# Expert weights stored tile by tile: one row of 8 KB per partition instead of two of 4 KB

## The chip, the core and the metric

The kernel runs on one core of one Trainium2 chip. The metric is the device time of one execution in microseconds (us). Three runs of the kernel before took 1865.32, 1869.44 and 1870.21 us; the median, 1869.44 us, is what is compared.

## What is computed

Two layers of a token mixer and a mixture of experts, for 512 latent tokens and 256 context tokens of width 1024, in float32. Almost all of the bytes that the kernel reads are the experts' weights. Cut to that part, the reference is:

```python
def expert_choice_ffn(xn, w_router, w_gate, w_up, w_down):
    cap = EC_CAPACITY_FACTOR * n // N_EXPERTS
    aff = jax.nn.softmax(jnp.einsum('bnd,de->bne', xn, w_router), axis=-1)
    gate, idx = lax.top_k(jnp.swapaxes(aff, 1, 2), cap)
    xs = xn[bidx, idx]
    hid = jax.nn.silu(jnp.einsum('becd,edf->becf', xs, w_gate)) * jnp.einsum('becd,edf->becf', xs, w_up)
    ys = jnp.einsum('becf,efd->becd', hid, w_down) * gate[..., None]
    return jnp.zeros_like(xn).at[bidx, idx].add(ys)
```

There are 16 experts per layer, each with three matrices of 1024 x 1024 (4 MB each): 2 x 16 x 12 MB in all. Each expert takes 64 latent tokens. In the first layer it also takes 32 context tokens; the last layer computes latent tokens alone.

## The kernel before

Experts are worked on in eight pairs per layer. A matrix of one expert comes in four tiles of 1 MB: tile i holds rows 256 i to 256 i + 255, two rows per partition (row 256 i + p and row 256 i + 128 + p in partition p). One pair therefore takes 24 tiles: four for each of three matrices and two experts.

The tiles of a layer stand in one list, `wq` (L1129 to L1132), in the order in which they are used: gate and up of pair 0, then for each pair gate of the next, down of this one, up of the next. `load_experts` (L1135) issues the loads on SP's DMA queue in that order, each into the next of a ring of buffers, `wreg`, and it issues one as soon as the tile that had the buffer is used up. In the last layer there are 16 buffers of 8 KB per partition: nine from L1128, six that come free at L1191 and one at L1710. In the first layer the ring is made of the four of L1191 and those added at L1715. The loads of the first tiles start before the routing is known.

`wide` (L1419) is the product of a pair with one matrix: for each of the four tile pairs, the latent tokens' matmuls (L1433), a filler, the context tokens' matmuls in the first layer (L1443), then `load_experts` again. The fillers are small pieces of other work put in between by hand: transposes and token gathering of the next pair (L1379, L1382), transposes of the hidden values (L1485), the scattering of the results (L1498, L1499).

Two stretches are special. The last down product of the last layer, `down_last` (L1662, matmuls at L1693), takes its weights by columns instead: each of the last two experts' down matrices comes as four tiles of 256 columns, so that a partition takes eight rows of 1 KB (L1138 to L1143; the fourth tile comes in two halves). And in the first layer the results of the first six pairs are added up in device memory by POOL's scattering DMAs (L1537), and read back once, also on POOL's queue (`collect`, L1546 and L1548), for transposes at L1554 and L1566 that stand as fillers among the matmuls of the last pairs. PE works strictly in order, so that a filler that waits holds up the matmuls behind it.

`layout` (L1763) arranges the inputs on the host, before the measured time. It passes the experts' matrices on as they are. The DMA engines' shares: 16 engines move each tile together, and an engine's record in the trace is a packet.

Of the kernel before, what the change touches and what calls it, by code (L numbers as in the profile page):

```python
# [14 lines left out]
D = 1024  # L15
KB = 8
# [3 lines left out]
E = 16  # L20
# [135 lines left out]
def build(nc, tc, xT, ctxT, params, w_ada, w_gates, w_in, w_out, w_router, w_e_gate, w_e_up, w_e_down,  # L156
# [3 lines left out]
    pe, act, dve, pool, sp = nc.tensor, nc.scalar, nc.vector, nc.gpsimd, nc.sync  # L160


    def body(A, RB, PS, scr, xrow, acc):
# [3 lines left out]
        def V(reg, *shape, dt=F32, off=0):  # L167
            n = 1
            for s in shape:
                n *= s  # L170
            k = 2 if dt == BF16 else 1
            assert off + n // k <= reg[1], (off, n, reg)
            ap = reg[2].tile[:, reg[0] + off:reg[0] + off + n // k]
            if dt == BF16:
                ap = ap.bitcast(dt)
            if len(shape) > 1:
                names = "abcdefg"[:len(shape)]
                ap = ap.rearrange("p (" + " ".join(names) + ") -> p " + " ".join(names),
                                  **{names[i]: shape[i] for i in range(1, len(shape))})
            return ap  # L180

        def B(i):
            return PS[:, i, :]
# [86 lines left out]
        def after(inst, firsts, how=mybir.DependencyClass.Sync):  # L270

            for f in firsts:
                tc.add_manual_dep(inst.ins, f.ins.name, mybir.DependencyInfo(how, mybir.DependencyReason.DATA),
                                  reason="its turn comes later")
# [122 lines left out]
        for l in range(2):  # L397
# [198 lines left out]
            for s in seqs:  # L596
                o, n = OFF[s], LEN[s]
# [5 lines left out]
            for q in range(4):  # L603
                sl = slice(32 * q, 32 * q + 32)
                src, dst = B(4 + LAT)[sl], G[sl, TC:TT]
                if q % 2:
                    src = src.rearrange("p (r w) -> p r w", r=8)
# [376 lines left out]
            for part in (('v', 'ga') if l == 0 and not GA0 else ('ga', 'v')):  # L984
                if part == 'ga':
# [18 lines left out]
                    for b in range(2):  # L1004
                        for t in range(CONV_K):
                            wcol = pc(l, P_CW + b * CONV_K + t)
                            o, i = CL_[:, b, w0:w1], Y[:, b, w0 + t:w1 + t]
# [37 lines left out]
            for b in range(2):  # L1045
                ps = in_block(FB + b, outs)
                for s in outs:
                    hf = LEN[s] // 2
                    f = FT[:, OFF[s]:OFF[s] + LEN[s]]
# [85 lines left out]
            def load_experts(firsts=(), most=1000):  # L1135
                while len(wtiles) < min(wtaken[0] + len(wreg), len(wq), most):
                    w, e, i = wq[len(wtiles)]
                    if last and w is w_e_down and e >= E - 2:  # L1138
                        t = V(wreg[len(wtiles) % len(wreg)], KB, 256)
                        src = w[l, e].rearrange("(k p) f -> p k f", p=128)[:, :, i * 256:i * 256 + 256]  # L1140

                        for k0, k1 in ((0, KB),) if i < 3 else ((0, 4), (4, KB)):
                            sp.dma_start(t[:, k0:k1], src[:, k0:k1])  # L1143
                    else:
                        t = V(wreg[len(wtiles) % len(wreg)], 2, D)
                        r = sp.dma_start(t, w[l, e].rearrange("(q a p) f -> q p a f", p=128, a=2)[i])
                        after(r, firsts)
                    wtiles.append(t)

# [11 lines left out]
            for db in range(KB):  # L1161
                h, lo = next_w()
                if last:

                    load_experts(wloads[-1:], 2 * db + 2)
                banks = in_banks()
                product(h, lo, YT, outs, banks, YORDER)
                if db == 1:

                    for s in outs:  # L1170
                        p = B(6 + s)[:, 0:16]
                        for k in range(KB):
                            pe.matmul(p, MOD[l][:, s, 24 + k:25 + k].to_broadcast([128, 128]), WR[:, k, 0:16],
                                      start=k == 0, stop=k == KB - 1)
                        dve.tensor_copy(SHR[:, s], p)
                for s in outs:
                    dve.scalar_tensor_tensor(X[s][:, db], banks[s], MOD[l][:, s, 16 + db:17 + db], X[s][:, db],
                                             op0=OP.mult, op1=OP.add)
                if db == 4:
                    ride(0)  # L1180
                for s in outs:
                    sq = sqs[s, db] = V(trs[s].next(), LEN[s])
                    act.activation(sq, X[s][:, db], AF.Square)
                if db == KB - 2:
                    warm(AF.Sqrt, sq[:, 0:1])
# [4 lines left out]
            wp = wp_open()  # L1190
            wreg += wp if last else wp[:4]  # L1191
            load_experts()


# [16 lines left out]
            for s in reversed(outs):  # L1211
                o, n = OFF[s], LEN[s]
# [27 lines left out]
            p = B(3)  # L1240
# [17 lines left out]
            for c in range(cs0, 6):  # L1258
# [3 lines left out]
                for hf in range(2):  # L1262
                    p = B((0, 1, 4)[n_ev % 3])
# [481 lines left out]
        for k in range(KB):  # L1745
            t = V(tring.next(), TL)
# [16 lines left out]
def layout(inputs):  # L1763
    f = lambda n: np.ascontiguousarray(np.asarray(inputs[n]))
    z = np.zeros
    col = lambda v: v.reshape(-1, 128).T
    a = {}
    a["xT"] = np.ascontiguousarray(f("x")[0].T)
    a["ctxT"] = np.ascontiguousarray(f("ctx")[0].T)
    par = z((128, NP_ALL), np.float32)  # L1770
    w_in = f("w_in")
    bg, cw = f("b_gates"), f("conv_w")
    wg = z((2, 128, KB, 32), np.float32)
    for l in range(2):
        o = l * NPAR
        par[:, o + P_BADA:o + P_BADA + 48] = col(f("b_ada")[l])
        par[:, o + P_G1:o + P_G1 + 8] = col(f("g_norm1")[l])
        par[:, o + P_G2:o + P_G2 + 8] = col(f("g_norm2")[l])
        par[:, o + P_GHN:o + P_GHN + 4] = col(f("g_hnorm")[l])
        for b in range(2):  # L1780
            par[:, o + P_CW + b * CONV_K:o + P_CW + (b + 1) * CONV_K] = cw[l][:, b * 128:b * 128 + 128].T
        par[:, o + P_CB:o + P_CB + 2] = col(f("conv_b")[l])
        par[:, o + P_LNG:o + P_LNG + 2] = col(f("conv_ln_g")[l])
        par[:, o + P_LNB:o + P_LNB + 2] = col(f("conv_ln_b")[l])
        for d in range(2):
            for h in range(H):
                for j in range(2):
                    r = d * 64 + (h // 2) * 32 + h % 2 + 2 * j
                    par[r, o + P_BG] = bg[l, h, 2 * d + j]
                    wg[l, :, :, 4 * (r // 32) + r % 32] = w_in[l][:, 1536 + h * 4 + 2 * d + j].reshape(KB, 128).T  # L1790
    par[:, P_GF:P_GF + 8] = col(f("g_final"))
    par[:, P_C:P_C + 8] = col(f("c")[0])
    par[:, P_C + 8:P_C + 16] = col(f("c_ctx"))
    a["params"] = par
    a["w_ada"] = f("w_ada")
    a["w_gates"] = wg.reshape(2, 128, KB * 32)
    cols = np.concatenate([w_in[:, :, :1536], w_in[:, :, 1552:]], axis=2)
    a["w_in"] = np.ascontiguousarray(cols.reshape(2, KB, 128, 22, 128).transpose(0, 3, 2, 1, 4)).reshape(2, 22, 128, KB * 128)
    a["w_out"] = np.ascontiguousarray(f("w_out").reshape(2, KB, 128, KB, 128).transpose(0, 3, 2, 1, 4)).reshape(2, KB, 128, KB * 128)
    wr = z((2, 128, KB, 32), np.float32)  # L1800
    wr[..., :E] = f("w_router").reshape(2, KB, 128, E).transpose(0, 2, 1, 3)
    a["w_router"] = wr
    for n in ("w_e_gate", "w_e_up", "w_e_down"):
        a[n] = f(n)

    def dft(n, scale):
        k = np.outer(np.arange(n), np.arange(n)) % n
        th = 2 * np.pi * k / n
        return np.cos(th) * scale, np.sin(th) * scale


    for name, n in (("dft_l", TL), ("dft_c", TC)):
        c, s = dft(n, 1.0 / np.sqrt(n * 64.0))
        hf, nf = n // 2, n // 256
        t = z((128, nf * 2 * hf + hf + 1))
        t[:, 0:nf * (hf + 1)] = c[:hf, :hf + 1].reshape(nf, 128, hf + 1).transpose(1, 0, 2).reshape(128, -1)
        t[:, nf * (hf + 1):nf * 2 * hf] = -s[:hf, 1:hf].reshape(nf, 128, hf - 1).transpose(1, 0, 2).reshape(128, -1)
        t[0, nf * 2 * hf:] = c[hf, :hf + 1]
        a[name] = t.astype(np.float32)
    c, s = dft(64, 1.0)  # L1820
    ch = z((128, 256))
    for g in range(2):
        ch[g * 64:g * 64 + 64, g * 64:g * 64 + 64] = c
        ch[g * 64:g * 64 + 64, 128 + g * 64:128 + g * 64 + 64] = s
    a["dft_ch"] = ch.astype(np.float32)
    return a
# [15 lines left out]
```

## Time and profile before

| | |
|---|---|
| runs, us | 1865.32, 1869.44, 1870.21 (median 1869.44) |
| the profiled execution, us | 1872.25, of it the span from the first to the last instruction 1870.5 |
| granted TensorE clock, mean | 0.973 |
| PE busy | 1749.7 us, 94% of the span |
| DVE, ACT, POOL busy | 34%, 24%, 9% |
| moved by DMA | 529.59 MB, 283 GB/s over the span |
| SP's DMA queue | 136960 packets, 459.66 MB |
| POOL's DMA queue | 18624 packets, 68.17 MB |
| expert stage, first layer | about 484 to 1040 us |
| expert stage, last layer | about 1371 to 1852 us |

Times in the views are counted in us from the start of the span. A row of a timeline or of the chain that gathers several instructions (x32) begins at its first and lasts to the end of its last. Matmuls overlap one another, and their ends are modelled; a matmul of 512 columns in these stages shows 0.59 us while the next one begins 0.21 or 0.43 us after it. In a timeline, brackets give the idle time of the engine before the row and what ended it. The granted clock is 1.00 at 2.4 GHz.

### The profile page before, as it was taken

What the parts mean: (1) busy time and instruction counts of PE and PEld (TensorE: products, weight loads), DVE (VectorE), ACT (ScalarE), POOL (GpSimd) and SP (SyncE); (2) the same over time, 40 slices, a digit from 0 to 9 for tenths busy, and PEclk for the clock granted to TensorE, in tenths of its full rate; (3) what the DMA queues carried; (4) which work ended last, traced back from release to release, by engine and by line L of the source; (5) the groups of instructions that cost most, each with busy time, mean ns of one, the idle gap of its engine ahead of it and who ended that gap; (6) DMA issues with size and microseconds to landing.
All of it is one profiled execution on the core that took longest, in us unless ns stands there. A gap on an engine that the chain in (4) does not pass through costs nothing.

```text
span 1870.5 us, 27692 instructions
## 1 busy us (share of the span) xinstructions
PE 1749.7 (94%) x11728; PEld 946.8 (51%) x11728; DVE 628.4 (34%) x1384; ACT 449.0 (24%) x862; POOL 165.3 (9%) x193
## 2 busy tenths in 40 slices
PE   6989999799899999999999989889889999999997
PEld 2768887576333333333333567777643444434433
DVE  4633897322201001001113668855321122111213
ACT  4432454312201101111010552445311010100001
POOL 1022221221101101100100001110000000000000
PEclk8999999899999999999999999999999999999998
DMA  9366344855999999999996122244669999999993
GB/s 343 102 203 197 99 131 154 303 196 196 349 409 393 393 409 394 394 408 394 392 408 243 34 74 68 68 110 152 271 252 409 408 409 408 409 408 409 409 390 123
DMA packets 155708, 529.59 MB, mean 283 GB/s; under 512 B 10176, under 2 KB 29632, under 8 KB 155584
## 3 DMA queue, kind: packets, MB, share of 16 engines
q1 hardware_dynamic: 136960, 459.66, 63.4%
q0 software_dynamic: 18624, 68.17, 11.6%
q8 instruction: 92, 1.51, 0.3%
q14 instruction: 32, 0.26, 0.0%
HBM read 513.10 MB, written 14.68 MB: 282 GB/s over the span
## 4 chain that ended last, share of the span: by engine, by line
PE 71%; DMA 10%; DVE 9%; issue 5%; ACT 2%; SPq 1%; POOL 1%; DVEq 0%; POOLq 0%; ACTq 0%
PE PS L1433 30%; PE PS L490 16%; PE PS L1443 8%; PE PS L1379 3%; DVE A L1015 2%; PE PS L1498 2%; DMA A<-w_e_up 2%; DMA WP<-w_e_up 2%; PE PS L284 1%; DMA A<-w_e_gate 1%; PE PS L1693 1%; DMA WP<-w_e_gate 1%; DMA accc<-A 1%; SPq L309 1%; PE PS L1485 1%
## 5 line engine op out<-in xcount | busy, mean ns | idle before, releaser
L490 PE MATMUL PS<-RA,RB 128*128 128x512 f32 (+1 forms) x2352 | 518.1, 368 | 23.6 <-ACT A L973 7.7
L1433 PE MATMUL PS<-A 128*32 128x512 f32 (+1 forms) x2256 | 432.6, 597 | 10.4 <-DMA A<-w_e_up 4.3
L490 PEld LDWEIGHTS PS<-RA,RB 128*128 128x128 f32 x2352 | 380.4, 195 | 100.0 <-issue 21.2
L1433 PE MATMUL PS<-WP,A 128*32 128x512 f32 (+1 forms) x2160 | 377.7, 596 | 2.2 <-DMA WP<-w_e_up 2.0
L1433 PEld LDWEIGHTS PS<-A 128*32 128x32 f32 (+1 forms) x2256 | 127.0, 122 | 237.9 <-issue 215.6
L1433 PEld LDWEIGHTS PS<-WP,A 128*32 128x32 f32 (+1 forms) x2160 | 110.1, 117 | 195.0 <-issue 179.7
L1443 PE MATMUL PS<-WP,A 128*32 128x512 f32 x816 | 113.2, 595 | 0.0
L1015 DVE SCALAR_TENSOR_TENSOR A<-A 128x783 f32<-128x783 f32 (+1 forms) x120 | 107.5, 923 | 0.1
L1499 DVE SCALAR_TENSOR_TENSOR A<-PS,A 128x512 f32<-128x512 f32 x80 | 57.5, 747 | 133.2 <-PE PS L1498 133.2
L1387 ACT ACTIVATE A<-PS,A 128x128 f32<-128x128 f32 x80 | 36.4, 458 | 267.2 <-DVE A L1389 266.8
L1486 ACT ACTIVATE A<-PS 128x512 f32<-128x512 f32 x40 | 23.8, 597 | 308.1 <-PE PS L1485 307.9
L1389 DVE TENSOR_SCALAR A<-PS,A 128x128 f32<-128x128 f32 x80 | 32.6, 409 | 184.7 <-PE PS L1382 102.7
L422 ACT ACTIVATE RB<-A 128x1024 fp32r<-128x1024 f32 x60 | 63.4, 1058 | 129.1 <-PE PS L490 82.8
L1443 PE MATMUL PS<-A 128*32 128x512 f32 x656 | 93.5, 596 | 0.0
L1532 DVE TENSOR_SCALAR A<-PS,A 128x512 f32<-128x512 f32 x6 | 4.5, 750 | 247.4 <-PE PS L1433 247.4
L282 POOL DMA_DIRECT2D A<-w_ada x80 | 60.1, 755 | 209.1 <-PE PS L284 133.7
L1506 DVE SCALAR_TENSOR_TENSOR RB<-PS,A,RB 128x512 fp32r<-128x512 f32 x18 | 13.5, 751 | 169.0 <-ACT RB L1505 168.1
L425 DVE TENSOR_TENSOR RB<-A,RB 128x1024 fp32r<-128x1024 f32 x50 | 60.9, 1222 | 21.2 <-ACT RB L422 20.9
L1379 PE MATMUL PS<-A 128*128 128x128 f32 x512 | 62.6, 281 | 5.0 <-DVE A L1499 4.5
L1379 PEld LDWEIGHTS PS<-A 128*128 128x128 f32 x512 | 59.5, 195 | 12.9 <-DVE A L1499 9.8
L1443 PEld LDWEIGHTS PS<-WP,A 128*32 128x32 f32 x816 | 27.2, 109 | 50.4 <-issue 49.6
L1498 PE MATMUL PS<-RB 128*128 128x512 f32 x160 | 51.6, 431 | 1.0 <-DVE A L1499 0.4
(334 smaller groups left out, 1575.2 us busy)
## 6 DMA issues: line engine op xcount, KB each, us to landing
A<-w_e_gate SPq DMA_DIRECT2D x75, 1024.0 KB, 18.5
A<-w_e_up SPq DMA_DIRECT2D x66, 1024.0 KB, 18.5
WP<-w_e_down SPq DMA_DIRECT2D x63, 1024.0 KB, 18.4
A<-w_e_down SPq DMA_DIRECT2D x63, 1024.0 KB, 18.6
WP<-w_e_up SPq DMA_DIRECT2D x62, 1024.0 KB, 18.4
WP<-w_e_gate SPq DMA_DIRECT2D x53, 1024.0 KB, 19.0
A<-w_ada POOLq DMA_DIRECT2D x80, 512.0 KB, 5.5
A<-w_in SPq DMA_DIRECT2D x44, 512.0 KB, 3.6
```

Of the source, the lines that this page charges most:

```text
L282: after(eng.dma_start(w, src[r, hf, k]), firsts if hf == 0 and k < len(ring.regs) else ())
L422: whi.append(act.activation(h, raw[i], AF.Copy))
L425: wlo.append(eng.tensor_tensor(lo, raw[i], h.bitcast(F32), OP.subtract))
L490: pe.matmul(banks[s][:, :LEN[s]], w[:, k], xin[:, j, k, OFF[s]:OFF[s] + LEN[s]], start=k == k0 and i == 0, stop=k == k1 and i == 2)
L1015: dve.scalar_tensor_tensor(o, i, wcol, o, op0=OP.mult, op1=OP.add)
L1379: pe.matmul(b[:, j], XT[2 + c][:, db * 128:db * 128 + 128], onehots[i][:, c], start=c == 0, stop=c == 3)
L1387: act.activation(dst[:, db], b[:, j], AF.Identity, bias=sh_, scale=sc_)
L1389: dve.tensor_scalar(dst[:, db], b[:, j], sc_, sh_, op0=OP.mult, op1=OP.add)
L1433: pe.matmul(B(o + hf)[c:c + wd, :], lhs(k, e)[:, c % 64:c % 64 + wd], w[e][:, a, hf * 512:hf * 512 + 512], start=k == 0, stop=k == KB - 1, ...
L1443: pe.matmul(B(o + 2)[32 * g:32 * g + 32, :], lhsc(k, e), w[e][:, a, hf * 512:hf * 512 + 512], start=k == 0, stop=k == KB - 1, tile_positio ...
L1498: pe.matmul(b, YS[:, j, db * 128:db * 128 + 128], PM if pm is None else pm, start=j == 0, stop=j == 1)
L1499: dve.scalar_tensor_tensor(X[LAT][:, db], b, MOD[l][:, LAT, 40 + db:41 + db], X[LAT][:, db], op0=OP.mult, op1=OP.add)
```

## The change

In device memory each expert's matrix is stored tile by tile: for each tile and each partition the two rows of 4 KB stand side by side, so that a partition's part of a tile is one run of 8 KB. The tiles of the last two experts' down matrix in the last layer are stored by their 256 columns, so that there, too, a partition's part is one run of 8 KB. What arrives in the buffers is what arrived before. The fourth of these column tiles is still loaded in two halves.

```diff
@@ -1137,13 +1137,13 @@
                     w, e, i = wq[len(wtiles)]
                     if last and w is w_e_down and e >= E - 2:
                         t = V(wreg[len(wtiles) % len(wreg)], KB, 256)
-                        src = w[l, e].rearrange("(k p) f -> p k f", p=128)[:, :, i * 256:i * 256 + 256]
+                        src = w[l, e, i].rearrange("p (k c) -> p k c", k=KB)
 
                         for k0, k1 in ((0, KB),) if i < 3 else ((0, 4), (4, KB)):
                             sp.dma_start(t[:, k0:k1], src[:, k0:k1])
                     else:
                         t = V(wreg[len(wtiles) % len(wreg)], 2, D)
-                        r = sp.dma_start(t, w[l, e].rearrange("(q a p) f -> q p a f", p=128, a=2)[i])
+                        r = sp.dma_start(t, w[l, e, i].rearrange("p (a f) -> p a f", a=2))
                         after(r, firsts)
                     wtiles.append(t)
 
@@ -1801,7 +1801,10 @@
     wr[..., :E] = f("w_router").reshape(2, KB, 128, E).transpose(0, 2, 1, 3)
     a["w_router"] = wr
     for n in ("w_e_gate", "w_e_up", "w_e_down"):
-        a[n] = f(n)
+
+        a[n] = np.ascontiguousarray(f(n).reshape(2, E, 4, 2, 128, D).transpose(0, 1, 2, 4, 3, 5)).reshape(2, E, 4, 128, 2 * D)
+
+    a["w_e_down"][1, E - 2:] = f("w_e_down")[1, E - 2:].reshape(2, KB, 128, 4, 256).transpose(0, 3, 2, 1, 4).reshape(2, 4, 128, 2 * D)
```

## Rows read from the trace of the kernel before

**Rows 1.** The page: busy tenths in 40 slices of 46.8 us, PE and DMA.

```profile
PE   6989999799899999999999989889889999999997
...
DMA  9366344855999999999996122244669999999993
```

**Rows 2.** Stretch: length, busy PE, PEld, DVE, ACT, POOL (instructions), clock, DMA share, GB/s.

```profile
1593.00:1815.00 222.00, 210.64 (x999) 87.82 (x998) 39.65 (x70) 19.96 (x35) 0.00 (x0) 1.00 1.03 408
```

**Rows 3.** Chain of work in order of time: start us, length us, what; last layer.

```profile
1514.61 3.84 PE PS L1379 x32
...
1571.46 3.84 PE PS L1379 x32
...
1631.03 3.84 PE PS L1379 x32
...
1692.97 3.84 PE PS L1379 x32
...
1754.37 3.84 PE PS L1379 x32
```

**Rows 4.** Timeline of weight loads into PE, last pair: start, length, engine, line, what.

```profile
1791.47 0.13 PEld L1433 LDWEIGHTS PS<-A 128*64 128x64 f32 x1 [1.60 <-DMA A<-w_e_down]
...
1796.58 0.20 PEld L1433 LDWEIGHTS PS<-A 128*64 128x64 f32 x4 [2.31 <-DMA A<-w_e_up]
...
1801.71 0.20 PEld L1433 LDWEIGHTS PS<-A 128*64 128x64 f32 x4 [2.35 <-DMA A<-w_e_up]
```

**Rows 5.** DMA from 1400 to 1500 us: packets, MB, rate, packets by size.

```profile
DMA packets 10591, 40.89 MB, mean 409 GB/s; under 512 B 620, under 2 KB 620, under 8 KB 10587
```

**Rows 6.** DMA from 1815 to 1825 us, the last eight tiles (1 KB rows).

```profile
DMA packets 3402, 3.45 MB, mean 345 GB/s; under 512 B 49, under 2 KB 3401, under 8 KB 3401
```

**Rows 7.** DMA from 15 to 20 us: w_ada, rows of 1 KB.

```profile
DMA packets 1936, 1.93 MB, mean 385 GB/s; under 512 B 56, under 2 KB 1936, under 8 KB 1936
```

**Rows 8.** DMA, 1260 to 1272 us: SP's queue (packets, MB, share); issues (KB, us to landing).

```profile
q1 hardware_dynamic: 560, 2.23, 57.5%
...
A<-w_out SPq DMA_DIRECT2D x2, 512.0 KB, 3.5
A<-w_e_up SPq DMA_DIRECT2D x1, 1024.0 KB, 6.0
A<-dft_l SPq DMA_DIRECT2D x1, 640.5 KB, 4.9
```

**Rows 9.** Last down product: timeline of PE and SP; on the page, that load's landing.

```profile
1827.61 1.94 PE L1693 MATMUL PS<-WP,A 128*64 128x256 f32 x8 [1.15 <-DVE RB L1700]
...
1846.06 1.94 PE L1693 MATMUL PS<-A 128*64 128x256 f32 x8
...
1826.52 2.88 SPq L1143 DMA_DIRECT2D A<-w_e_down  x2
...
A<-w_e_down SPq DMA_DIRECT2D x2, 512.0 KB, 8.6
```

**Rows 10.** Timeline of PE in the first layer's expert stage.

```profile
721.59 4.29 PE L1433 MATMUL PS<-A 128*32 128x512 f32 x32
...
733.29 4.74 PE L1433 MATMUL PS<-WP,A 128*32 128x512 f32 x32
...
740.29 3.62 PE L1433 MATMUL PS<-WP,A 128*32 128x512 f32 x32
...
932.14 0.63 PE L1554 MATMUL PS<-A 128*128 128x128 f32 x4 [0.49 <-DMA A<-accl]
...
938.32 5.04 PE L1433 MATMUL PS<-A 128*32 128x512 f32 x28 [2.85 <-DMA A<-w_e_gate]
```

**Rows 11.** Stretch of 4 us after that wait, columns as in rows 2.

```profile
938.00:942.00 4.00, 3.68 (x24) 1.01 (x26) 0.00 (x0) 0.00 (x0) 0.00 (x0) 0.60 1.03 410
```

**Rows 12.** DMA from 925 to 930 us: SP's queue (q1) and POOL's (q0).

```profile
q1 hardware_dynamic: 270, 1.04, 52.4%
q0 software_dynamic: 233, 0.95, 48.9%
```

## The prediction

> **What bounds the kernel now.** I read the 40 slices first: from slice 31 to slice 38 PE is at 9 and the DMA engines are at 9 too, so the busy shares decide nothing there [rows 1]. That is the expert stage of the second layer. Its stretch from 1593 to 1815 us has PE busy for 210.6 of 222 us and the DMA engines at a share of 1.03, moving 408 GB/s [rows 2]. Which of the two is late is read from the chain of work in order of time. A group of 32 token-gathering matmuls (L1379) comes once per pair of experts. From 1514.61 to 1571.46 the distance is 56.85 us: that is PE's own pace, with no wait on a tile. The next three distances are 59.57, 61.94 and 61.40 us [rows 3]. One pair takes 24 tiles of 1 MB; at 409 GB/s a tile takes 1.0486 / 0.409 = 2.564 us, and 24 take 61.5 us [rows 5]. So this layer begins bound by PE, lives on the 16 tiles loaded beforehand, and from about 1571 us goes at the pace of the loads. PE has lost 182.91 - 3 x 56.85 = 12.4 us by 1754.37, and in the last pair weight loads wait another 1.60 + 2.31 + 2.35 = 6.3 us for tiles, a little of which is their usual gap [rows 4]. Together about 18 us lie there, and no more can be won there by faster loads.
>
> In the first layer's expert stage PE does more work per tile (context tokens too), and waits on tiles are few. A step of 32 matmuls takes 3.62 us; two take 4.29 and 4.74 us, and before 938.32 PE stands idle for 2.85 us and then needs 5.04 us for 28 matmuls instead of 28/32 x 3.62 = 3.17, with a granted clock of 0.60 over the four us after the idle time [rows 10, 11]. That is 0.67 + 1.12 + 2.85 + 1.87 = 6.5 us, and 0.49 us at 932.14 for the sums that are read back.
>
> **The change, part by part.** *Same bytes, same tiles, same order.* For 376 of the 384 tiles the bytes that reach a partition and the place they go to are the same; only their place in device memory moves. The number of load instructions, waits and buffers doesn't change, and the layout is made on the host, outside the measured time. These parts cost nothing and need no cover.
>
> *Does a row of 8 KB travel as one packet?* The trace of before has no such load. It shows the next best thing: between 1260 and 1272 us two DMAs of 4 KB rows (one w_out, one expert tile) and the table dft_l, with 5124 bytes per partition, land. Their packets must be 128 + 256 + 128 + 16 x 3 completion packets = 560, and 560 are recorded, 2.23 MB [rows 8]. (The second w_out is issued too late to land.) Had the 5124-byte rows been cut at 4 KB there would be 688. w_out is written with an inner size of 512 bytes and still goes as 4 KB packets, so dimensions that lie side by side are merged. So I take it that a tile goes as 128 packets instead of 256.
>
> *What a packet costs.* Each engine carries 1/16 of a tile. With 4 KB rows, 16 packets in 2.564 us are 160.2 ns each [rows 5]. The last eight tiles are read in rows of 1 KB: 345 GB/s, 3.039 us for 64 packets, 47.5 ns each [rows 6]. A straight line through both: 36.7 ps per byte and 9.9 ns per packet. At 8 KB that gives 310.5 ns, 2.484 us per tile, 422 GB/s: 0.080 us less. The other 1 KB rows, of w_ada, go at 385 GB/s (42.6 ns each) [rows 7]; a line through those gives 3.4 ns per packet, 317.0 ns at 8 KB, 2.536 us per tile: 0.028 us less. If a packet cost nothing at all beyond the first line's bytes, a tile would take 2.405 us: 0.159 us less. Below zero the price is the third rival. I take 0.080: the 1 KB rows of the tail belong to the same tensor and queue, and a partition's successive rows lie 512 KB apart in both, as the 4 KB rows do now, while w_ada's lie 2 KB apart.
>
> The Trainium skill (DMA: Bandwidth & Descriptors, "Where 436 GB/s comes from") says that from HBM to SBUF the HBM side binds at about 358 GB/s, which would leave nothing to the size of a row. The trace disagrees: 409 GB/s. The same section knows a load of 16 MB at 425 GB/s; by that a tile would take an estimated 2.467 us, 0.097 less, and the second layer would gain 16 us.
>
> *Second layer.* 16 of its 192 tiles are in place before its first matmul, and the last eight belong to the last down product. So the last tile that PE waits for is the 168th of the stream, which runs without a pause (409 GB/s in its first part, 408 in its last [rows 2, 5]). PE still frees buffers faster (56.85 / 24 = 2.37 us per tile) than 2.484, so the stream stays full. Gain: 168 x 0.080 = 13.4 us, below the 18 us there; ends 168 x 0.028 = 4.7 and the full 18.
>
> *The last eight tiles.* Their rows go from 1 KB to 8 KB (six tiles) or two of 4 KB (two tiles): at least 3.039 - 2.564 = 0.475 us less for each. I cost that at nothing: the last down product waits for VectorE, not for a tile, and the last halves, issued at 1826.52, land 8.6 us later, by 1838, before their matmuls at 1846.06 [rows 9]. After the change both come earlier. If that cover went, 8 us would have to be used up first.
>
> *First layer.* By 721 us some 90 tiles have passed, each 0.080 us earlier: 7 us, against 1.8 us of waits, so those go. At 938 us another 80 tiles have passed, 6 us, against 2.85 + 1.87. But something else is late there: PE waits at 932.14 for the read-back of the accumulated sums, on POOL's queue. While both queues are busy they take turns packet by packet: 270 of SP's with 52.4% of the time, 233 of POOL's with 48.9% [rows 12]. A turn of SP's becomes 150 ns longer (310.5 - 160.2). The first MB read back needs 16 packets per engine, 2.4 us more if each waits a whole turn; I put the scatters before it in the same queue at as much again, an estimate. So PE can lose up to 4.8 us more at 932 instead of 4.7 at 938. First layer: 1.8 us if the tiles are faster, 1.8 + 4.7 = 6.5 at most. I take 3.
>
> **Sum:** 13.4 + 3 = 16.4 us. The profiled execution took 1872.25 us (1870.5 of span, 1.75 around it), so 1855.9 us by it; it lies 2.8 us above the median of 1869.44, which gives **1853.0 us**, 0.9% faster. Ends: 4.7 + 1.8 = 6.5 (1863) and 18 + 6.5 = 24.5 (1845).
>
> **The rivals.** *1. The line through w_ada is right* (0.028 us per tile): 8 us with 3 us of the first layer, 1861 us. For it: a line through 1 KB rows that lie close together. Against it: it mixes rows that lie close with rows that lie 512 KB apart.
>
> *2. A packet over 4 KB is no cheaper per byte*, or is cut in two on its way. Then each tile takes 2.564 us as now and the time is 1869 us. For it: nothing in the trace shows the rate of a packet over 4 KB, only that one exists [rows 8]. Against it: the cost per packet between 1 KB and 4 KB. The Trainium skill (DMA: Bandwidth & Descriptors, "SWDGE vs HWDGE vs iDMA") bears on this: a packet is best at 4096 bytes or less. If more is no use, this rival holds; no run here shows it yet.
>
> *3. Slower: device memory serves the new rows worse.* Neighbouring engines' shares start 32 KB apart instead of 16 KB, and where rows lie matters: 1 KB rows go at 345 GB/s in one place and 385 in another [rows 6, 7]. At 400 GB/s a tile takes 2.621 us, 0.057 more; both layers pass it on, since both are late on tiles already: (168 + 170) x 0.057 = 19 us, 1889 us. It decides from 5.6 / 338 = 0.017 us per tile, 406 GB/s, down. Against it: the new rows are longer and run on without a jump.
>
> **How the numbers follow.** The forecast 0.62 (1846 to 1858), PE alone as the bound with nearly all of both layers' waits gone, about 1845, 0.03; rival 1: 0.10; rival 2: 0.15; rival 3: 0.10. What a measurement of this kernel can tell from no change is about 0.3%, 5.6 us: faster holds the first three cases but for 0.02 of rival 1, so 0.73; same is rival 2 and that 0.02, 0.17; slower 0.10. The range of 1845 to 1871 leaves out rival 3 and a little at the fast end.
>
> **What would show it.** Right: SP's queue moves 136960 - 376 x 128 - 6 x 896 - 2 x 768 = 81920 packets; 1400 to 1600 us goes at some 420 GB/s; the L1379 groups lie 57 to 60 us apart to the end; the steps of 4.29 and 4.74 us are gone. Wrong: packets fewer but 409 GB/s (rival 2), a rate under 406 (rival 3), a wait at L1554 longer than the one that went at 938 (first layer), or waits on tiles in the last down product.

## The result, and the profile after

| | before | changed |
|---|---|---|
| median of 11 runs, us | 1869.44 | 1860.82 |
| lowest and highest | 1865.32 to 1877.42 | 1848.85 to 1864.63 |
| the profiled execution, us (its span) | 1872.25 (1870.5) | 1857.74 (1856.0) |

The ratio is 0.9944, with a 95% interval of 0.9928 to 0.9960: the change makes the kernel 0.56% faster, 8.6 us where 16.4 were forecast. The two profiled executions lie 14.5 us apart, since that of before happens to lie above its median and that of after below its own. So the profiles can say where time went, but not, by their sum, how much it is.

The page of the changed kernel, its busy tenths, rates and SP's queue (packets, MB, share of 16 engines):

```profile
PE   7899999899899999999999989889989999999997
...
DMA  9365344855899999999995112233659999999992
GB/s 346 115 208 193 106 133 137 314 188 209 350 419 402 411 412 403 399 421 391 393 393 217 35 54 79 76 108 129 250 240 421 420 420 421 420 421 420 421 420 99
...
q1 hardware_dynamic: 81920, 459.66, 61.8%
```

SP's queue moves the same bytes in 81920 packets, which is exactly the number forecast. In the last layer, slices 31 to 39, it moves 420 to 421 GB/s. DMA from 1400 to 1500 us, where [rows 5] had 409:

```profile
DMA packets 5768, 42.04 MB, mean 420 GB/s; under 512 B 640, under 2 KB 640, under 8 KB 640
```

None of the data packets is under 8 KB any more. A tile takes 1.0486 / 0.420 = 2.497 us (2.564 before), and a packet of 8 KB 312.1 ns of an engine.

The chain of work in the last layer, the gathering matmuls that come once per pair, as in [rows 3]:

```profile
1511.78 3.84 PE PS L1379 x32
...
1568.61 3.84 PE PS L1379 x32
...
1625.48 3.84 PE PS L1379 x32
```

and PE's timeline for the last two of them, with the first matmuls of the last down product:

```profile
1682.34 3.84 PE L1379 MATMUL PS<-A 128*128 128x128 f32 x32 [0.38 <-DVE A L1499]
...
1741.92 3.84 PE L1379 MATMUL PS<-A 128*128 128x128 f32 x32 [0.38 <-DVE A L1499]
...
1804.02 1.94 PE L1693 MATMUL PS<-A 128*64 128x256 f32 x8
```

The distances are 56.83, 56.87, 56.86 and 59.58 us. PE now keeps its own pace of 56.85 us for two pairs more than before, and where the tiles set the pace it is 59.6 us instead of 59.6 to 61.9. Two waits of weight loads for tiles are left in the last pair, where [rows 4] had three:

```profile
1782.57 0.20 PEld L1433 LDWEIGHTS PS<-A 128*64 128x64 f32 x4 [1.72 <-DMA A<-w_e_up]
...
1787.54 0.20 PEld L1433 LDWEIGHTS PS<-A 128*64 128x64 f32 x4 [2.20 <-DMA A<-w_e_up]
```

The first layer looks different. PE's timeline there, around the read-back of the sums (compare [rows 10]):

```profile
923.38 3.62 PE L1433 MATMUL PS<-A 128*32 128x512 f32 x32
931.31 1.09 PE L1554 MATMUL PS<-A 128*128 128x128 f32 x4 [4.31 <-DMA A<-accl]
932.33 3.64 PE L1443 MATMUL PS<-A 128*32 128x512 f32 x16
935.74 4.03 PE L1433 MATMUL PS<-A 128*32 128x512 f32 x32
```

Waits on tiles are gone from PE there. In their place PE waits 4.31 us for the first part of the read-back, where it waited 0.49 before. Stretches of 4 us around it, columns as in [rows 2]:

```profile
928.00:932.00 4.00, 0.69 (x4) 0.71 (x4) 0.00 (x0) 0.00 (x0) 0.00 (x0) 0.72 1.01 407
932.00:936.00 4.00, 4.00 (x22) 0.99 (x24) 0.75 (x1) 0.00 (x0) 0.00 (x0) 0.50 1.01 407
936.00:940.00 4.00, 4.00 (x35) 1.01 (x28) 0.00 (x0) 0.00 (x0) 0.00 (x0) 0.93 1.05 427
```

After standing idle the engine works at 1.2 GHz for a while (a granted clock of 0.50): 16 matmuls of L1443 take 3.64 us, which take 1.92 elsewhere. The read-back itself is late. These are POOL's scatters and the read-back, before and changed (the two starts), and in the changed kernel the read-back's time from issue to landing:

```profile
L1537 POOL DMA_INDIRECT accl<-A x2: 1408/1410/1411, 906.0 to 914.0; - x2
L1546 POOL DMA_DIRECT2D A<-accl x2: 841/854/866, 921.3 to 922.2; - x2
...
L1537 POOL DMA_INDIRECT accl<-A x2: 1407/1408/1410, 901.4 to 910.1; - x2
L1546 POOL DMA_DIRECT2D A<-accl x2: 841/852/863, 918.1 to 918.9; - x2
...
DMA to landing us min/median/max: 13.1/13.1/13.1
```

From the first of these scatters to the read-back's issue it takes 16.7 us, where it took 15.3. The first MB lands 13.1 us after its issue, where it took 10.7. Together that is 3.8 us, as much as PE's wait has grown (4.31 against 0.49). DMA from 925 to 930 us, both queues, beside [rows 12]:

```profile
q1 hardware_dynamic: 183, 1.34, 66.3%
q0 software_dynamic: 182, 0.68, 34.2%
```

Before, the two queues had 52.4% and 48.9% of the time. Now SP's has two thirds and POOL's one third, with as many packets each: by these counts they still take turns packet by packet, but SP's packets are twice as long.

The stages can be laid beside each other by the first matmuls of each. For the changed kernel (a line's instructions with durations, first and last start):

```profile
L1433 PE MATMUL PS<-WP,A x96: 592/592/1063, 481.8 to 497.2; 128*32 128x512 f32 x96
L1621 PE MATMUL PS<-A x48: 592/592/617, 1008.2 to 1035.2; 128*32 128x512 f32 x48
L1433 PE MATMUL PS<-A x72: 592/592/643, 1368.1 to 1388.8; 128*64 128x512 f32 x72
L1693 PE MATMUL PS<-A x32: 379/379/430, 1804.0 to 1836.6; 128*64 128x256 f32 x32
```

The first layer's last down product begins at L1621, so that the column "between" starts with that product. Read in the same way for all kernels of this study, in us (one profiled execution each):

| kernel | up to the first expert | first layer's, up to its last down | between | last layer's, up to its last down | rest |
|---|---|---|---|---|---|
| before | 484.1 | 528.2 | 358.6 | 447.6 | 52.0 |
| changed | 481.8 | 526.4 | 359.9 | 435.9 | 52.0 |
| the same once more | 487.6 | 523.7 | 360.8 | 436.3 | 51.0 |
| 4 KB rows, side by side | 487.7 | 525.6 | 357.7 | 448.1 | 51.3 |
| 2 KB rows, side by side | 485.9 | 553.9 | 357.3 | 472.9 | 51.0 |
| 8 KB in the last layer only | 486.3 | 524.7 | 358.1 | 435.8 | 51.0 |
| 8 KB in the first layer only | 489.6 | 526.4 | 360.9 | 447.6 | 51.8 |
| changed, last eight tiles in 1 KB | 484.5 | 525.4 | 357.9 | 436.3 | 51.1 |
| changed, read-back used later | 489.3 | 518.9 | 358.6 | 436.9 | 51.5 |
| before, read-back used later | 482.6 | 530.2 | 359.3 | 448.4 | 52.0 |
| changed, first layer's last two pairs in 4 KB | 482.3 | 519.0 | 359.5 | 436.0 | 51.0 |
| both of these | 485.4 | 519.9 | 358.4 | 437.2 | 51.0 |

The stretch up to the first expert, which the change touches only by the first loads, goes from 481.8 to 489.6 us without order, up to 5.8 us between two executions of one kernel. The last layer's stage repeats to within 1.5 us, and it is 11 to 12 us shorter than before. The first layer's stage is 1.8 us shorter than before in these two profiles, which is less than the spread among executions: its first step alone, which starts at the lower clock (0.50 from 480 to 484 us in the changed kernel), takes between 4.1 and 5.7 us in different kernels:

```profile
484.12 5.16 PE L1433 MATMUL PS<-WP,A 128*32 128x512 f32 x32
...
481.77 5.73 PE L1433 MATMUL PS<-WP,A 128*32 128x512 f32 x32
...
489.31 4.09 PE L1433 MATMUL PS<-WP,A 128*32 128x512 f32 x32
```

The rows are from the kernel before, the changed kernel, and the changed kernel with the read-back used later.

### The profile page after: what moved, and what is told of

Read it like the earlier page. It is cut to its first block, busy times and chain, and to the rows that moved or that the text cites. A ratio compares the mean times of both kernels' runs of the same rounds, so it can differ in the third digit from the quotient of the medians.

```text
span 1856.0 us, 27692 instructions
## 1 busy us (share of the span) xinstructions
PE 1744.3 (94%) x11728; PEld 947.8 (51%) x11728; DVE 627.9 (34%) x1384; ACT 448.5 (24%) x862; POOL 166.0 (9%) x193
## 3 DMA queue, kind: packets, MB, share of 16 engines
q1 hardware_dynamic: 81920, 459.66, 61.8%
## 4 chain that ended last, share of the span: by engine, by line
PE 70%; DMA 10%; DVE 9%; issue 5%; ACT 2%; SPq 2%; POOL 1%; another core or an unknown queue 0%; DVEq 0%; POOLq 0%; ACTq 0%
PE PS L1433 29%; PE PS L490 16%; PE PS L1443 8%; PE PS L1379 3%; DVE A L1015 2%; PE PS L1498 2%; PE PS L284 1%; PE PS L1693 1%; SPq L309 1%; DMA accc<-A 1%; DMA WP<-w_e_up 1%; DMA A<-w_e_up 1%; DMA A<-w_e_down 1%; DMA A<-w_e_gate 1%; DMA WP<-w_e_gate 1%
## 5 line engine op out<-in xcount | busy, mean ns | idle before, releaser
L1433 PE MATMUL PS<-A 128*32 128x512 f32 (+1 forms) x2256 | 428.1, 594 | 2.7 <-DMA A<-w_e_up 2.2
L1433 PE MATMUL PS<-WP,A 128*32 128x512 f32 (+1 forms) x2160 | 373.9, 597 | 0.7 <-DMA WP<-w_e_up 0.7
L1433 PEld LDWEIGHTS PS<-A 128*32 128x32 f32 (+1 forms) x2256 | 128.0, 121 | 224.9 <-issue 213.7
L1433 PEld LDWEIGHTS PS<-WP,A 128*32 128x32 f32 (+1 forms) x2160 | 107.0, 117 | 192.7 <-issue 187.6
L1443 PE MATMUL PS<-WP,A 128*32 128x512 f32 x816 | 112.5, 595 | 0.0
L1443 PE MATMUL PS<-A 128*32 128x512 f32 x656 | 95.3, 607 | 0.0
L1506 DVE SCALAR_TENSOR_TENSOR RB<-PS,A,RB 128x512 fp32r<-128x512 f32 x18 | 13.5, 750 | 163.7 <-ACT RB L1505 162.8
L1443 PEld LDWEIGHTS PS<-WP,A 128*32 128x32 f32 x816 | 26.8, 109 | 50.8 <-issue 50.8
```

The source lines that it names most:

```text
L1433: pe.matmul(B(o + hf)[c:c + wd, :], lhs(k, e)[:, c % 64:c % 64 + wd], w[e][:, a, hf * 512:hf * 512 + 512], start=k == 0, stop=k == KB - 1, ...
L1443: pe.matmul(B(o + 2)[32 * g:32 * g + 32, :], lhsc(k, e), w[e][:, a, hf * 512:hf * 512 + 512], start=k == 0, stop=k == KB - 1, tile_positio ...
```

## The experiments

**Which part of the change makes loads faster: fewer packets, or no jump?** In the old layout the two rows of a partition lie 512 KB apart; in the new one they follow each other. This kernel keeps them together, but leaves 512 bytes after each, so that they stay two packets:

```diff
-                        r = sp.dma_start(t, w[l, e, i].rearrange("p (a f) -> p a f", a=2))
+                        r = sp.dma_start(V(wreg[len(wtiles) % len(wreg)], 2, 1024), w[l, e, i][:, :, 0:1024])
...
+        v = np.zeros((2, E, 4, 128, 2, 1152), np.float32)
+        v[..., :1024] = a[n].reshape(2, E, 4, 128, 2, 1024)
```

> A partition's two rows of a tile stand side by side as in the changed kernel, but with 512 bytes of nothing after each, so that they travel as two packets of 4 KB with no jump of 512 KB between them (also in the last eight tiles). Theory (what a load costs is its number of packets): 16 packets per engine and tile, 409 GB/s between 1400 and 1600 us, and the time of the kernel before, 1869 us within 4. Rival (the gain comes from the jump that is gone, not from the packets): 420 GB/s and the time of the changed kernel, 1861 us.

It took 1870.48 us, a ratio of 0.9992 (0.9972 to 1.0012) to the kernel before. DMA from 1400 to 1500 us:

```profile
DMA packets 10597, 40.91 MB, mean 409 GB/s; under 512 B 622, under 2 KB 622, under 8 KB 10593
```

Same rate, same time and, but for a few at the edges of the stretch, the same packets as before: a jump of 512 KB costs no more than a gap of 512 bytes. The rival has fallen.

**The price of a packet.** The same with four rows of 2 KB (512 floats and 128 of nothing after each).

> Every tile as four rows of 2 KB per partition, side by side with 512 bytes of nothing after each: twice the packets of the kernel before. The 4 KB packets (160.2 ns) and the 8 KB packets of the changed kernel (2.497 us a tile, 312.1 ns) lie on a line of 37.1 ps per byte and 8.3 ns per packet. Theory (a fixed price per packet): 84.3 ns at 2 KB, 2.70 us a tile, 389 GB/s, and both layers at the pace of the loads: about 168 x 0.13 us in the last layer and as much in the first, 1905 to 1915 us. Rival (between 2 KB and 4 KB nothing changes; only the step above 4 KB was special): 409 GB/s and 1870 us.

It took 1921.96 us, a ratio of 1.028 (1.0243 to 1.0316), 55 us more and 7 us above the range that was expected. DMA from 1500 to 1600 us:

```profile
DMA packets 19434, 38.66 MB, mean 387 GB/s; under 512 B 587, under 2 KB 587, under 8 KB 19429
```

At 387 GB/s a packet takes 84.7 ns; the line had 84.3. Both layers are 25 us longer: a tile takes 0.146 us more (2.710 against 2.564), and 168 x 0.146 = 24.5. So the packets of 2, 4 and 8 KB lie on one line of 8.3 ns per packet and 37.1 ps per byte, and nothing special happens at 4 KB. The rows of 1 KB in [rows 6] lie near it as well (47.5 ns against 46.3); those of w_ada in [rows 7] (42.6) do not, and why is open.

**Which layer carries the gain?** One kernel has the new layout in the last layer only, one in the first only. The old order of bytes is read through a view:

```diff
-                        r = sp.dma_start(t, w[l, e, i].rearrange("p (a f) -> p a f", a=2))
+                        old = w[l, e, i].rearrange("(a h) (g f) -> (h g) a f", a=2, g=2)
+                        r = sp.dma_start(t, old if l == 0 else w[l, e, i].rearrange("p (a f) -> p a f", a=2))
...
+        a[n][0] = f(n)[0].reshape(E, 4, 128, 2 * D)
```

> The new layout in the last layer alone; the first layer's tiles stand and travel as before. From the two profiles the last layer's stage (first tile's matmul to the first of the last down product) went from 447.6 to 435.9 us. Theory (the last layer carries the gain): 11 to 12 us below the kernel before, 1857 to 1858. Rival (the first layer gives half of the gain, by sending tiles earlier): 1863 or more.

It took 1860.22 us, 11.3 below the 1871.54 of the kernel before on the same chip (ratio 0.9943, 0.9926 to 0.9959).

The other has `l == 1` in that place, and its last eight tiles in rows of 1 KB at their old places.

> The new layout in the first layer alone; the last layer as before, with its 1 KB rows at the end. From the two profiles the first layer's stage (first tile's matmul to the last down product) went from 534.6 to 532.8 us: 5 to 6 us of waits on tiles gone, 4.3 us of wait at the read-back come. Theory: 1 to 3 us below the kernel before, 1867, which can't be told from none. Rival (in most executions the longer wait at the read-back costs more than the waits that went): 2 to 4 us above it, 1872; that would explain why the changed kernel gains 8.6 us by the medians and 14.5 between the two profiles.

It took 1874.56 us, 3.0 above the kernel before (ratio 1.0020, 1.0006 to 1.0033). The last layer alone gives the whole gain and more, and the new layout in the first layer alone is a small loss, the rival of what was expected: 11.3 - 3.0 = 8.3, close to the 8.6 us of the change. The wait at the read-back is there in its profile as well (us in total, times, longest):

```profile
PE PS L1555 <- DMA A<-accl: 4.3, 1, 4.3
```

**Is it the read-back?** Here the transposes of the sums go to PE one product later, so that it need not wait for them at that place:

```diff
-                if p >= NACC:
-                    scat += late
-                    late.clear()
                 if p + 1 < NP:
                     fetch_pair(p + 2)
                     gate(p + 1, lambda q: (pop(scat), q and pop(trans)))
+                if p >= NACC:
+                    scat += late
+                    late.clear()
```

> The changed kernel, with the transposes of the sums that are read back given out one product later (from the down product of the seventh pair on instead of the gate product of the eighth), so that PE need not wait for the read-back at 932 us. Theory (the wait of 4.3 us there, and the matmuls at a granted clock of 0.5 after it, some 2.5 us, are lost time): 5 to 7 us below the changed kernel, 1854 to 1856. Rival (PE then waits for a tile instead, as before the change, or for VectorE where the transposes now come eight at a time): within 2 us of the changed kernel.

It took 1853.93 us, a ratio of 0.9908 (0.9886 to 0.9930) to the kernel before. PE's timeline and the granted clock at that place:

```profile
929.28 3.62 PE L1433 MATMUL PS<-A 128*32 128x512 f32 x32
932.71 1.90 PE L1443 MATMUL PS<-A 128*32 128x512 f32 x16
934.43 3.62 PE L1433 MATMUL PS<-A 128*32 128x512 f32 x32
...
932.00:936.00 4.00, 4.00 (x44) 1.17 (x36) 0.00 (x0) 0.00 (x0) 0.00 (x0) 1.00 1.01 407
```

No wait, no fall of the clock, and no wait on a tile instead: the stage takes 518.9 us, 7.5 less than in the changed kernel. Of these, 1.6 us lie in the stage's first step (4.09 against 5.73), which has nothing to do with the read-back; the other 5.9 are what the edit gives in this profile. By the two ratios (0.9908 and 0.9944) it is 6.7 us.

The same edit in the kernel before tells whether the obstacle was there all along.

> The kernel before, with only the transposes of the read-back sums given out one product later. It tells whether the 6 to 7 us that this won in the changed kernel need the new rows. Theory (before, PE waits at that place for a tile, not for the read-back, and the tiles are as late as ever): within 2 us of the kernel before. Rival (the read-back was the obstacle in both): 5 us or more below it.

It took 1872.49 us, a ratio of 1.0029 (1.0010 to 1.0049), so it loses 5.4 us, more than the 2 us that were allowed for, and gains nothing. Its timeline:

```profile
936.76 4.94 PE L1433 MATMUL PS<-A 128*32 128x512 f32 x28 [4.05 <-DMA A<-w_e_gate]
```

With the old rows PE runs into the missing tile at the same place, and its wait is longer by as much as it comes earlier (4.05 us against 2.85 in [rows 10]). The read-back is the obstacle only when the tiles are faster.

**Is it the length of a turn?** In the changed kernel, the tiles of the first layer's last two pairs, which are loaded while the sums are read back, travel again as two packets of 4 KB:

```diff
-                        r = sp.dma_start(t, w[l, e, i].rearrange("p (a f) -> p a f", a=2))
+                        old = w[l, e, i].rearrange("(a h) (g f) -> (h g) a f", a=2, g=2)
+                        r = sp.dma_start(t, old if l == 0 and e >= E - 4 else w[l, e, i].rearrange("p (a f) -> p a f", a=2))
```

> The changed kernel, but in the first layer the tiles of the last two pairs, which are loaded while the sums are read back, travel as two packets of 4 KB as before. Theory (the two queues take turns packet by packet, and a longer packet of SP's makes POOL's queue wait longer): the first MB of the read-back lands after 10.7 us as before the change and not 13.1, the wait at L1554 falls from 4.3 to 2 us or less, and the time is 2 to 5 us below the changed kernel. Rival (the read-back is late because PE comes earlier, or because all bytes together are too many): the wait stays near 4 us and the time is that of the changed kernel.

It took 1849.42 us, a ratio of 0.9895 (0.9865 to 0.9925) to the kernel before, and gains more on the changed kernel than the 2 to 5 us expected. The read-back (time from issue to landing) and PE's wait:

```profile
DMA to landing us min/median/max: 10.7/12.9/15.1
...
926.91 0.63 PE L1555 MATMUL PS<-A 128*128 128x128 f32 x4 [0.68 <-DMA A<-accl]
```

and the two queues from 920 to 925 us:

```profile
q1 hardware_dynamic: 264, 1.02, 51.6%
q0 software_dynamic: 244, 1.00, 51.1%
```

The turns are even again, the first MB lands 10.7 us after its issue as before the change, and PE waits 0.68 us. The tiles in flight there go as the old packets, and PE waits for none of them in this profile; that the six pairs of faster tiles before them are the reason was not tested by itself. PE comes to the read-back no later than in the changed kernel, and the two queues together move no fewer bytes (403 GB/s from 920 to 925 us here, 404 from 925 to 930 there), so the cause of the wait is the length of SP's packets. This version beats the kernel before and, by its ratio (0.9895 against 0.9944 and, once more, 0.9931) and by the stage, the changed one.

**The last eight tiles.** The changed kernel with these in rows of 1 KB as before:

> The changed kernel, but the last eight tiles in rows of 1 KB at their old places. Theory (the last down product never waits for a tile): within 2 us of the changed kernel, 1860 to 1862. Rival (the end of the stream sets the end): 3 to 5 us above it (eight tiles, 0.5 us each).

It took 1855.45 us, a ratio of 0.9936 (0.9913 to 0.9960) to the kernel before, against 0.9944 for the change. The time itself lies below what was expected, as does the kernel before on that chip (1867.05). That part of the change is worth nothing that can be measured.

**The changed kernel once more, and both remedies together.**

> The changed kernel once more, beside the two best versions and on the same chip. Theory (the parts add up: 11.3 us won by the last layer alone, 3.0 us lost by the first alone): 8 to 9 us below the kernel before; in its profile the first layer's stage takes 525 to 527 us with a wait of about 4 us at L1554, the last layer's 436 us. Rival (the gain of 14.5 us between the first two profiles is the true one): 13 us or more below.

It took 1859.11 us, 10.6 below the kernel before on that chip (ratio 0.9931, 0.9905 to 0.9956), a little more than expected. Its first layer's stage takes 523.7 us, with a wait of 3.9 us at L1554; that is shorter than expected, 1.5 us of it by the stage's first step (4.22 against 5.73). The interval is 8 to 18 us below, so this run alone does not exclude the rival's 13 us. That of the first measurement is 7.5 to 13.5. Both together leave 8 to 13 us for the change; the two medians say 8.6 and 10.6.

> Rows of 8 KB except for the first layer's last two pairs, and the transposes of the read-back given out one product later as well. Theory (either of the two alone already takes the wait at the read-back away): the first layer's stage takes 518 to 519 us as with either alone, and the time is within 2 us of the version with 4 KB rows in those pairs, 17 to 20 us below the kernel before. Rival (they take away different waits): 3 us or more below that version.

It took 1852.80 us, 16.9 below the kernel before (ratio 0.9901, 0.9873 to 0.9928), with 519.9 us in the first layer. That is no more than the 17.6 us of the 4 KB rows alone. The two take away the same wait, and either alone is enough.

## Why the prediction came out as it did

**Right: what bounds the last layer.** The stream of tiles set the pace from 1571 us on, and a faster stream gave its time to PE. The 18 us of waits were not used up: the stage went from 447.6 to 435.9 us. What is left is 59.58 - 56.85 = 2.7 us in the pair before the last, and 1.72 + 2.20 = 3.9 us of weight loads waiting in the last, a little of which is their usual gap.

**Right: one packet per partition, with a price per packet.** 81920 packets were counted. Rival 2, that a packet over 4 KB is no cheaper per byte, fell at 420 GB/s, and rival 3 with it. The Trainium skill (DMA: Bandwidth & Descriptors, "SWDGE vs HWDGE vs iDMA") holds a packet best at 4096 bytes or less. For the rate of a stream the measurement differs: 8 KB packets are 2.7% faster than those of 4 KB (420 against 409 GB/s). Beside another queue the longer packets have a price, as the read-back shows. Rival 1, through w_ada's rows, asked for 413 or 414 GB/s and is wrong too. That the measured 1860.82 us is its 1861 is chance: the last layer gave more than it said, and the first less.

**A little large: the gain per tile.** The line through 1 KB and 4 KB gave 0.080 us per tile; it is 0.067. The 47.5 ns of the 1 KB rows, read from a stretch of 10 us, lie 1.2 ns above the line that 2, 4 and 8 KB share, and that made the price of a packet 9.9 instead of 8.3 ns. By the measured value 168 tiles give 11.3 us, and that is what the last layer gave by itself. Here 13.4 us had been forecast: the mechanism was right and the term was 2 us too large.

**Wrong: the first layer, 3 us forecast, no clear gain or a small loss found.** The step that failed is the choice within the range from 1.8 to 6.5 us, and in it one term that was put at nothing: the slow clock behind the new wait. The read-back was bounded at 4.8 us more of waiting, and 3.8 us more came, for the reason given, the longer turn: 2.4 us in the landing of the first MB, as forecast, and 1.4 in the scatters before it, put at another 2.4. The sign that the prediction had named for it, a wait at L1554 longer than the one that went at 938, is there (4.31 against 2.85). But the sum counted 1.87 us for the slow clock after the old wait as a gain, and not that PE would fall to 1.2 GHz after the new one: L1554, L1443 and L1433 behind it take (1.09 - 0.63) + (3.64 - 1.92) + (4.03 - 3.62) = 2.6 us longer. So 3.8 + 2.6 = 6.4 us came against the 6.5 that the prediction saw go. The lower end should have been zero or less.

The tile waits of the kernel before were also more than these 6.5 us. Some steps that the prediction did not list were late as well, for example this one (3.62 us when no tile is late):

```profile
856.35 4.01 PE L1433 MATMUL PS<-WP,A 128*32 128x512 f32 x32
```

Laid step by step beside the changed kernel, late tiles cost the stage 8.7 us before and nothing after. With 6.4 us at the read-back and 0.6 in the stage's first step (5.73 against 5.16) coming back, that is the 1.8 us by which the stage is shorter in these two profiles.

Nor does a wait always cost the clock. In the kernel with the new rows in the last layer only, PE waits 3.02 us for the same tile as before at the same place, the clock stays at 1.00, and the 28 matmuls take 3.63 us instead of the 5.04 of [rows 10]:

```profile
938.50 3.63 PE L1434 MATMUL PS<-A 128*32 128x512 f32 x28 [3.02 <-DMA A<-w_e_gate]
...
938.00:942.00 4.00, 3.50 (x28) 0.91 (x28) 0.00 (x0) 0.00 (x0) 0.00 (x0) 1.00 1.03 410
```

After the 3.8 to 4.4 us at the read-back the clock fell in all four profiles that have that wait, which cost 1.8 to 2.6 us.

That the first layer alone loses 3.0 us by the medians is not explained by its stage, which is as long as before in the four profiles with the new rows there (523.7 to 526.4, against 524.7 to 528.2 in three with the old). The stretch between the layers is 359.9 to 360.9 us in three of these four, and 357.7 to 358.6 in those three. That could be 1 or 2 us, but single executions differ by as much. The granted clock of all runs points the same way: its mean is 0.9710 with the new rows in the first layer only and 0.9736 in the kernel before on that chip, 0.9713 in the changed kernel, 0.9737 with the new rows in the last layer only or with the read-back used later. An estimate from the first two: 0.0026 x 1870 = 4.9 us of full clock are lost beyond those of the kernel before, and that is time wherever PE is at work. Where in the kernel, beyond the place of the wait, was not separated: this stays open.

**Right: what was costed at nothing.** The last eight tiles are covered by the last down product, as the run with 1 KB rows shows. The number of instructions is unchanged (27692).

The forecast of 1853.0 us was 7.8 us too low for 1860.82: 2 us of it from the size of the last layer's term, and 3 to 6 from the first layer, depending on whether that gave nothing or lost 3 us.

## What to carry to other kernels

Where a stream of loads sets the pace, the length of a partition's contiguous run in device memory is worth checking even at 4 KB, and a layout made on the host gets it without an instruction more. But where another queue's transfer is awaited beside the stream, longer packets take bandwidth from it: there keep the shorter rows, or use its result later. Price a new wait with the slow clock that can follow it, not by its length alone.

## What the runs showed of the hardware

A load on SP's queue at full stream costs each engine 84.7 ns for 2 KB, 160.2 for 4 KB and 312.1 for 8 KB: 387, 409 and 420 GB/s over 16 engines. A jump of 512 KB between a partition's rows costs no more than a gap of 512 bytes (409 GB/s with either). Two queues that are both busy had about equal numbers of packets, whether these were of 4 KB on both or of 8 KB on one (270 and 233 packets for 52.4% and 48.9% of the time before, 183 and 182 for 66.3% and 34.2% after). Not expected was how dear a wait of 4 us is for PE: another 1.8 to 2.6 us at the lower clock in four profiles. Behind a wait of 2.85 us in one profile the clock fell (0.60), behind one of 3.02 us in another it did not (1.00).
